# Branch A's queries and keys transposed two tiles at a time, and a later due time for the T5 set-up, in a hybrid encoder layer

## The chip, the cores and the metric

The kernel runs on one core of a Trainium2 chip. The metric is the device time of one execution in microseconds, as the median of several runs. A profiled execution gives the trace; its span goes from the first to the last instruction.

## The reference

One encoder layer is applied with the same weights to two inputs, a prompt of 512 tokens and a sample of 1024 tokens, 1024 wide, in f32. Cut to what matters here:

```python
h = rmsnorm(x, norm_g)
qa, ka, va, za, qb, kb, vb, zb, ga, gb = split(h @ w_in)
qa, ka = rmsnorm(qa per head, qn_a), rmsnorm(ka per head, kn_a)      # branch A: 8 heads of 64
oa = neighbourhood_attention(qa, ka, va, rpb_a) * silu(za)           # 8 x 16 window on a grid 64 wide
qb, kb = rmsnorm(qb per head, qn_b), rmsnorm(kb per head, kn_b)      # branch B: 8 heads, 2 key heads
ob = window_gqa_attention(qb, kb, vb, t5_table, sink_b) * silu(zb)   # |i-j| <= 128, T5 bias, sink logit
y = x + (sigmoid(ga) * (oa @ w_o_a) + sigmoid(gb) * (ob @ w_o_b)) @ w_out
```

## The kernel before

Every f32 product is made of three fp32r matmuls: an operand is split into a high part (an ACT copy to fp32r) and a low part (DVE or POOL subtract it), and hi x hi, hi x lo and lo x hi are added up in PSUM. The work goes in this order: norm of the prompt, attention of the prompt, its dense phase (gates, output projections, w_out), then attention and dense phase of the sample.

Tokens lie in tiles of 128: 4 for the prompt, 8 for the sample. An attention phase (`attention_phase`, line 648) goes through six groups: four of branch A with two heads each, two of branch B with four heads and one key head each. In a group, for each tile:

- `project` (line 728) makes queries, keys and values of the tile with 24 matmuls of 384 columns into one of two "p" banks (line 761). ACT squares (L780), DVE reduces (L785), POOL makes the reciprocal roots (L792, L799), ACT and DVE write the values in two parts into a tile `v` (L806, L809; 7 buffers for the sample, 6 for the prompt), and DVE scales queries and keys into `qk` (L816; 2 buffers).
- `make_qk` (line 847) transposes `qk` on PE into one "x" bank (line 861): two transposes of 128 columns for branch A (two heads' queries side by side, then their keys), three for branch B. Then ACT copies the keys with their gain (L882), DVE makes the low part (L887), ACT copies the queries (L896) and DVE makes their low part (L901). The prompt's branch A stores queries shifted by 64 tokens (`whole`), so that its first tile is written in two halves that lie apart.
- When the last tile that a block of 128 queries needs is there, the block waits in a list (line 1127); two blocks of branch A, or one of branch B, make a batch for `attend` (line 908): scores (L934), bias and running minimum on DVE (L969), exponentials on ACT (L978), scaling (L1008, L1010), transposes of the weights (L1026) and products with the values (L1063). A block of the sample reads the values of its own tile and both neighbours; one of the prompt, of two tiles.

`setup` (line 620), called on line 1644 with due time -0.7, loads the sink and makes its negative (L629), loads the T5 table and two constants (L634 to L636), makes the line of T5 biases by a matmul (L639) and a subtraction (L643), and stores it to DRAM (L646), from where branch B's groups load it (L708). The sink is named as an input of every score operation.

The order is written by a planner (`Flow.run`, line 207). Every operation has a list of engines with a fixed cost, a due time (`prio`) and what it depends on. The planner steps through time by these costs; an engine that is free takes, of the operations that are ready and whose buffers have room, the one with the lowest due time. What it finds is the order of each engine's queue. Loads and stores all go through SP's queue in that order, and a store waits there for its source. Branch A's due time is the running number of the tile in the phase; a group's weights are due 3 tiles before it.

Of the kernel before, what the change touches and what calls it, by code (L numbers as in the profile page):

```python
# [10 lines left out]
F32 = mybir.dt.float32  # L11
F32R = mybir.dt.float32r
AF = mybir.ActivationFunctionType
ALU = mybir.AluOpType
# [6 lines left out]
OADD = (("pool", 612), ("dve", 335))  # L21
DEBUG = 0
HB = 4
BANKS = {"p": 2, "x": 5, "d": 1}
ROTA = "ppxxxxxd"
FILL_P, FILL_S = 3, 2
# [14 lines left out]
P = 128  # L41
D = 1024
# [8 lines left out]
GW = 384  # L51
# [303 lines left out]
def encoder_kernel(  # L355
# [23 lines left out]
    nc = tc.nc  # L379
    act = nc.scalar  # L380
    dve = nc.vector
    pe = nc.tensor
# [7 lines left out]
    ident = cpool.tile([P, P], F32, tag="ident", name="ident")  # L390
# [25 lines left out]
    one = cpool.tile([1, P], F32, tag="one", name="one")  # L416
# [7 lines left out]
    ACT_ = lambda n, sbuf=True: (110 if sbuf else 68) + 0.832 * n  # L424
# [195 lines left out]
    def setup(pool, prio, after):  # L620
        raw = f.value(pool, [P, 8], F32, "sink_raw", 1)
        f.dma(lambda: nc.sync.dma_start(gcol, gains), 2048, -1, into=[gains_v])
        f.op(
            (("dve", 80),), lambda e: dve.tensor_scalar(gq, gcol[:, 0:2], -0.125, None, op0=ALU.mult),
            -1, use=[gains_v], into=[gains_v],
        )
        f.dma(lambda: nc.sync.dma_start(raw.t, sink.partition_broadcast(P)), 4096, prio, new=[raw], after=after)
        sink_v.writers.append(f.op(
            (("dve", 80),), lambda e: dve.tensor_scalar(nsink, raw.t, -1.0, None, op0=ALU.mult), prio, use=[raw]  # L629
        ))  # L630
        t5_sb = f.value(pool, [32, 8], F32, "t5_sb", 1)
        hot = f.value(pool, [32, 512], F32, "hot_sb", 1)
        far = f.value(pool, [8, 512], F32, "far_sb", 1)
        f.dma(lambda: nc.sync.dma_start(t5_sb.t, t5), 1024, prio, new=[t5_sb], after=after)  # L634
        f.dma(lambda: nc.sync.dma_start(hot.t, t5_hot), 65536, prio, new=[hot], after=after)
        f.dma(lambda: nc.sync.dma_start(far.t, t5_far), 16384, prio, new=[far], after=after)  # L636
        ps = bank("x")
        f.op(
            (("pe", 900),), lambda e: pe.matmul(ps.t[:8, :], t5_sb.t, hot.t, start=True, stop=True),  # L639
            prio, new=[ps], use=[t5_sb, hot],  # L640
        )
        f.op(
            (("dve", 602),), lambda e: dve.tensor_tensor(far.t, far.t, ps.t[:8, :], op=ALU.subtract),  # L643
            prio, use=[ps, far], into=[far],
        )
        line_op.append(f.dma(lambda: nc.sync.dma_start(line_d, far.t), 16384, prio, use=[far]))  # L646

    def attention_phase(geo, hh, hl, h_ops, mask_d, early, late):

        nb, nt = geo.nb, geo.nt  # L650
        kt = f.value(early, [P, 4, nt], F32R, "kt", 1)
        stores = {(c, n): [] for c in range(8) for n in range(nt // 512)}
        exps = []

        def tile_(shape, dt, tag, bufs):
            return f.value(early if tag in ("sq", "ss", "rs_v", "rs_r", "v", "q", "qt", "qk") else late, shape, dt, tag, bufs)
# [68 lines left out]
            o += i * GW if br == "B" else 0  # L725
            return nb_t.t[:, o : o + n]

        def project(br, w, t, prio):

            nq, nk = (2, 2) if br == "A" else (4, 1)  # L730
            nn = nq + nk
# [23 lines left out]
            for k in range(KC):  # L755
                hi, lo = w[k // 2]
                c = slice((k % 2) * GW, (k % 2) * GW + GW)
                for m, (u, mv) in enumerate(((0, hi), (0, lo), (1, hi))):
# [50 lines left out]
                lambda e: dve.tensor_tensor(vv(1), pv(), vv(0).bitcast(F32), op=ALU.subtract),  # L809
                prio, use=[ps, v], into=[v],  # L810
            )
            qk = tile_([P, GW], F32, "qk", 2)
            one = nn if br == "A" else nq
            f.op(
                (("dve", DVE_(one * 64)),),
                lambda e: dve.tensor_tensor(  # L816
                    qk.t[:, : one * 64].rearrange("p (h d) -> p h d", d=64),
                    ps.t[:, : one * 64].rearrange("p (h d) -> p h d", d=64),
                    r.t[:, :one].unsqueeze(2).to_broadcast([P, one, 64]),
                    op=ALU.mult,  # L820
                ),
                prio, new=[qk], use=[ps, r],
            )
            if br == "B":

# [18 lines left out]
            for j in range(nb)  # L844
        ]

        def make_qk(br, gi, t, qk, prio):

            npair = 1 if br == "A" else 2
            k0 = 2 * (gi % 2)  # L850
            pt = bank("x")
            whole = br == "A" and shifted
            if whole:
                q = q_whole.setdefault(gi, tile_([P, 2, nt + 64], F32R, "qt", 2))
            else:
                q = tile_([P, 2, 2 * P], F32R, "q", 4)
            fresh = not q.writers

            def emit(e):
                for i in range(npair + 1):  # L860
                    pe.transpose(pt.t[:, i * P : (i + 1) * P], qk.t[:, i * P : (i + 1) * P], ident)  # L861

            f.op((("pe", 110 * (npair + 1)),), emit, prio, new=[pt, q] if fresh else [pt], use=[qk])
            if fresh and not whole:
                q.writers.clear()
            n = npair * P
            pts = lambda: pt.t[:, :n]
            qv = lambda u: q.t[:, u, :n]
            if whole and t:
                qv = lambda u: q.t[:, u, t * P : (t + 1) * P]  # L870
# [4 lines left out]
            tok = slice(t * P, (t + 1) * P)  # L875
# [4 lines left out]
            a = f.op(  # L880
                (("act", ACT_(P) + 45),),
                lambda _: act.activation(kt.t[:, k0, tok], pk(), AF.Copy, scale=gain_k[br]),  # L882
                prio, use=[pt, gains_v], after=old, **kw,
            )
            b = f.op(
                (("dve", DVE_(P) + 165),),
                lambda _: dve.scalar_tensor_tensor(  # L887
                    kt.t[:, k0 + 1, tok], pk(), gain_k[br], kt.t[:, k0, tok].bitcast(F32), op0=ALU.mult, op1=ALU.subtract
                ),
                prio, use=[pt, gains_v], after=[a] + old, hold=[kt],  # L890
            )
            for s in slots:
                reads[s] = []
            c = f.op(
                (("act", ACT_(n) + 40),),
                lambda _: act.activation(qv(0), pts(), AF.Copy, scale=gain_q[br]),  # L896
                prio, use=[pt, gains_v], into=[q],
            )
            f.op(
                (("dve", DVE_(n) + 165),),  # L900
                lambda _: dve.scalar_tensor_tensor(  # L901
                    qv(1), pts(), gain_q[br], qv(0).bitcast(F32), op0=ALU.mult, op1=ALU.subtract
                ),
                prio, use=[pt], into=[q], after=[c],
            )
            return q, [a, b]

        def attend(br, gi, g, batch, nb_t, info, prio):
# [199 lines left out]
        for gi, (br, g) in enumerate(groups):  # L1108
# [524 lines left out]
    for t in range(gp.nb):  # L1633
# [4 lines left out]
        for i, (ps, users) in enumerate(gains_row if t == 0 else ()):  # L1638
# [133 lines left out]
```

## Time and profile before

| | us |
|---|---|
| median of 3 runs | 1148.09 (1146.76 to 1149.12) |
| profiled execution | 1146.52 |
| its span | 1144.7 |
| PE busy | 1133.8 |
| DVE busy | 854.4 |
| ACT busy | 644.9 |
| POOL busy | 308.3 |

A time beside an instruction counts from the start of the span. A matmul's row gives its start and its own duration, which overlaps with the next one's; the pace is read from start to start.

### The profile page before, as it was taken

The numbers are of one execution on the slowest core, as the hardware profiler recorded it, in microseconds if no ns is written. First come the engines' busy times: TensorE is split into PE (matmuls) and PEld (weight loads), VectorE is DVE, ScalarE is ACT, GpSimd is POOL, SyncE is SP. The second block draws the span as 40 slices with busy tenths as digits, with TensorE's granted clock in tenths as the row PEclk, the third lists the DMA queues.
The fourth block names the chain that finished last, engine by engine and source line by source line (L and its number), as shares of the span: only waits on it lengthen the run. The fifth ranks groups of instructions, "written<-read, shape, count | busy, mean of one in ns | idle before, by whom it ended". The sixth has DMA issues, their size and how long they took to land.

```text
span 1144.7 us, 18482 instructions
## 1 busy us (share of the span) xinstructions
PE 1133.8 (99%) x6139; PEld 985.8 (86%) x6139; DVE 854.4 (75%) x1975; ACT 644.9 (56%) x1467; POOL 308.3 (27%) x413
## 2 busy tenths in 40 slices
PE   8999999999999999999999999999999999999998
PEld 6999988888888899999999888888888888788887
DVE  5888798497765468887778888865878755497984
ACT  5777987544433346665678988865534434343320
POOL 3653433000010054343333445330222210132110
PEclk9999999999999999999999999999999999999999
DMA  7854543488786422121221213226657335573072
GB/s 253 273 158 141 181 113 102 115 264 266 232 277 199 165 72 67 25 70 32 71 61 50 56 37 93 56 66 214 218 148 211 129 111 159 200 238 121 29 223 90
DMA packets 124705, 159.86 MB, mean 140 GB/s; under 512 B 28297, under 2 KB 66961, under 8 KB 124610
## 3 DMA queue, kind: packets, MB, share of 16 engines
q1 hardware_dynamic: 124610, 158.69, 45.4%
q8 instruction: 48, 0.79, 0.3%
q14 instruction: 47, 0.39, 0.1%
HBM read 121.93 MB, written 41.44 MB: 143 GB/s over the span
## 4 chain that ended last, share of the span: by engine, by line
PE 94%; DVE 2%; DMA 2%; ACT 1%; POOL 1%; issue 0%; SPq 0%; ACTq 0%; POOLq 0%
PE p L761 25%; PE x L1285 9%; PE x L1286 9%; PE x L1284 9%; PE x L1063 5%; PE x L1026 5%; PE x L934 4%; PE p L1284 4%; PE p L1285 4%; PE d L1284 4%; PE p L1286 4%; PE d L1286 4%; PE d L1285 4%; PE x L861 2%; DMA ot<-u_d 1%; DMA w<-in_w_att_dram 1%
## 5 line engine op out<-in xcount | busy, mean ns | idle before, releaser
L761 PE MATMUL p<-whi,hh 128*128 128x384 f32 x384 | 133.4, 348 | 0.0
L761 PE MATMUL p<-wlo,hh 128*128 128x384 f32 x384 | 133.1, 347 | 0.0
L761 PE MATMUL p<-whi,hl 128*128 128x384 f32 x384 | 132.4, 345 | 0.0
L978 ACT ACTIVATE sb<-sb,mx 128x384 f32<-128x384 f32 (+1 forms) x192 | 107.5, 563 | 22.4 <-DVE mx L969 22.2
L1167 ACT ACTIVATE whi<-raw 128x512 fp32r<-128x512 f32 (+1 forms) x140 | 81.1, 590 | 52.6 <-PE x L1285 26.2
L761 PE MATMUL p<-whi,hb 128*128 128x384 f32 x384 | 107.5, 347 | 0.0
L1172 POOL TENSOR_TENSOR wlo<-raw,whi 128x512 fp32r<-128x512 f32 (+1 forms) x29 | 40.9, 1413 | 242.4 <-ACT whi L1167 130.4
L1284 PE MATMUL x<-hh,whi 128*128 128x512 f32 x264 | 102.7, 389 | 0.0
L1285 PE MATMUL x<-hl,whi 128*128 128x512 f32 x264 | 102.7, 389 | 0.0
L1286 PE MATMUL x<-hh,wlo 128*128 128x512 f32 x264 | 102.7, 389 | 0.0
L1037 DVE TENSOR_TENSOR pp<-x,pp 128x512 fp32r<-128x512 f32 (+1 forms) x136 | 82.6, 638 | 18.9 <-ACT pp L1032 17.8
L1172 DVE TENSOR_TENSOR wlo<-raw,whi 128x512 fp32r<-128x512 f32 (+1 forms) x111 | 70.1, 645 | 30.5 <-ACT whi L1167 30.2
L1285 PE MATMUL x<-T,whi 128*128 128x512 f32 x224 | 87.5, 390 | 0.3 <-DVE T L1172 0.2
L1286 PE MATMUL x<-T,wlo 128*128 128x512 f32 x224 | 87.2, 389 | 0.0
L1284 PE MATMUL x<-T,whi 128*128 128x512 f32 x224 | 87.1, 389 | 0.0
L1032 ACT ACTIVATE pp<-x 128x512 fp32r<-128x512 f32 (+1 forms) x136 | 70.9, 560 | 22.8 <-PE x L1026 21.8
L799 POOL TENSOR_TENSOR rs_r<-rs_v,mhalf 128x4 f32<-128x4 f32 (+1 forms) x72 | 81.7, 1134 | 5.7
L1063 PE MATMUL x<-pp,v 128*128 128x256 f32 (+1 forms) x368 | 77.8, 324 | 0.8 <-DVE pp L1037 0.8
L792 POOL TENSOR_SCALAR rs_v<-ss 128x4 f32<-128x4 f32 (+1 forms) x72 | 26.2, 364 | 187.3 <-DVE ss L785 184.6
L761 PEld LDWEIGHTS p<-whi,hl 128*128 128x128 f32 x384 | 73.0, 190 | 1.3 <-issue 1.0
L761 PEld LDWEIGHTS p<-wlo,hh 128*128 128x128 f32 x384 | 73.0, 190 | 1.0 <-issue 0.5
L761 PEld LDWEIGHTS p<-whi,hh 128*128 128x128 f32 x384 | 73.0, 190 | 0.9 <-issue 0.5
(351 smaller groups left out, 2985.5 us busy)
## 6 DMA issues: line engine op xcount, KB each, us to landing
raw<-in_w_g_dram SPq DMA_DIRECT2D x76, 256.0 KB
w<-in_w_att_dram SPq DMA_DIRECT2D x46, 384.0 KB
ot<-o_d SPq DMA_DIRECT2D x36, 256.0 KB
g_d<-C SPq DMA_DIRECT2D x34, 256.0 KB
raw<-in_w_z_dram SPq DMA_DIRECT2D x32, 256.0 KB
raw<-in_w_out_dram SPq DMA_DIRECT2D x32, 256.0 KB
C<-g_d SPq DMA_DIRECT2D x24, 256.0 KB
out_dram<-C SPq DMA_DIRECT2D x23, 256.0 KB
```

The costliest lines, as they stand in the source:

```text
L761: pe.matmul(ps.t[:, :GW], part[u](k), mv.t[:, c], start=k == 0 and m == 0, stop=k == KC - 1 and m == 2,)
L799: lambda e: nc.gpsimd.tensor_tensor(r.t[:, :nn], rv.t[:, :nn], mhalf[:, :nn], op=ALU.pow),
L978: act.activation(sb.t[:, :width], sb.t[:, :width], AF.Exp, bias=mx.t[:, i : i + 1], scale=-1.0, accum_out=sm.t[:, i : i + 1],)
L1026: pe.transpose(pt.t[:, u * P : (u + 1) * P], sbs[i].t[:, c * P : (c + 1) * P], ident)
L1032: lambda e, pt=pt, pp=pp, nn=nn: act.activation(pp.t[:, 0, :nn], pt.t[:, :nn], AF.Copy),
L1037: lambda e, pt=pt, pp=pp, nn=nn: dve.tensor_tensor(pp.t[:, 1, :nn], pt.t[:, :nn], pp.t[:, 0, :nn].bitcast(F32), op=ALU.subtract),
L1063: pe.matmul(out(), v.t[:, vs], mv(), start=first, stop=last)
L1167: (("act", ACT_(n)),), lambda e: act.activation(hi(), src(), AF.Copy), prio,
L1172: lambda e: engines[e].tensor_tensor(lo(), src(), hi().bitcast(F32), op=ALU.subtract), prio,
L1284: pe.matmul(out, hi.t[:, cs], mh(), start=first and k == 0, stop=False)
L1285: pe.matmul(out, hi.t[:, cs], ml(), start=False, stop=False)
L1286: pe.matmul(out, lo.t[:, cs], mh(), start=False, stop=last and k == len(ws) - 1)
```

## The change

Two neighbouring tiles of branch A share one `qk` tile of 512 columns, the second tile's queries and keys from column 256. The first tile of a pair is projected and no more; with the second, one run of four transposes follows (queries of both tiles, then keys of both), and one copy of 256 columns each for keys and queries in place of two of 128. For the prompt's first pair the query copy is in two parts, of 192 and 64 columns. Blocks that need either tile of the pair become ready with the second. The set-up is called with due time 9, and its two constants lie in one of the four `xt` buffers, which the norm uses, in place of two tiles of their own.

```diff
@@ setup
-        hot = f.value(pool, [32, 512], F32, "hot_sb", 1)
-        far = f.value(pool, [8, 512], F32, "far_sb", 1)
+        both = f.value(pool, [P, D], F32, "xt", 4)
+        hot, far = (lambda: both.t[:32, :512]), (lambda: both.t[:8, 512:1024])
...
-        line_op.append(f.dma(lambda: nc.sync.dma_start(line_d, far.t), 16384, prio, use=[far]))
+        line_op.append(f.dma(lambda: nc.sync.dma_start(line_d, far()), 16384, prio, use=[both]))
@@ project
-            qk = tile_([P, GW], F32, "qk", 2)
+            qk = beside or tile_([P, 512 if two else GW], F32, "qk", 2)
             one = nn if br == "A" else nq
+            c0 = 256 if beside else 0
...
-                    qk.t[:, : one * 64].rearrange("p (h d) -> p h d", d=64),
+                    qk.t[:, c0 : c0 + one * 64].rearrange("p (h d) -> p h d", d=64),
@@ make_qk
             def emit(e):
-                for i in range(npair + 1):
-                    pe.transpose(pt.t[:, i * P : (i + 1) * P], qk.t[:, i * P : (i + 1) * P], ident)
+                for i in range((npair + 1) * nt_):
+                    j = i // 2 + i % 2 * 2 if nt_ == 2 else i
+                    pe.transpose(pt.t[:, i * P : (i + 1) * P], qk.t[:, j * P : (j + 1) * P], ident)
...
-            n = npair * P
+            n, nk = npair * nt_ * P, nt_ * P
...
+            elif whole and nt_ == 2:
+
+                parts = [
+                    (lambda u: q.t[:, u, 64:n], lambda: pt.t[:, 64:n], n - 64),
+                    (lambda u: q.t[:, u, nt : nt + 64], lambda: pt.t[:, :64], 64),
+                ]
...
-            slots = [(s, t) for s in (k0, k0 + 1)]
+            tok = slice(t * P, t * P + nk)
+            slots = [(s, t + i) for i in range(nt_) for s in (k0, k0 + 1)]
...
-            pk = lambda: pt.t[:, n : n + P]
+            pk = lambda: pt.t[:, n : n + nk]
@@ attend
-                        at = runs[0][0] if whole else pair * P
+                        at = runs[0][0] if whole else runs[0][0] % (2 * P) if br == "A" and two else pair * P
@@ the loop over a group's tiles
-                v, qk = project(br, w, t, prio)
-                info[t] = (v, *make_qk(br, gi, t, qk, prio))
-                waiting += [b for b in (a_blocks if br == "A" else b_blocks) if max(b[1]) == t]
+                if br == "A" and two:
+                    if t % 2 == 0:
+                        v0, qk = project(br, w, t, prio)
+                        continue
+                    v, _ = project(br, w, t, prio, qk)
+                    made = make_qk(br, gi, t - 1, qk, prio, 2)
+                    info[t - 1], info[t], last = (v0, *made), (v, *made), (t - 1, t)
+                else:
+                    v, qk = project(br, w, t, prio)
+                    info[t], last = (v, *make_qk(br, gi, t, qk, prio)), (t,)
+                waiting += [b for b in (a_blocks if br == "A" else b_blocks) if max(b[1]) in last]
@@ the call
-    setup(norm_p, -0.7, h_ops["p"][1][:1])
+    setup(norm_p, 9, h_ops["p"][1][:1])
```

## Rows read from the trace of the kernel before

**Rows 1.** The page's part 1: busy us (share of the span) and instructions.

```profile
PE 1133.8 (99%) x6139; PEld 985.8 (86%) x6139; DVE 854.4 (75%) x1975; ACT 644.9 (56%) x1467; POOL 308.3 (27%) x413
```

**Rows 2.** The page's part 4: the chain that ended last, by engine.

```profile
PE 94%; DVE 2%; DMA 2%; ACT 1%; POOL 1%; issue 0%; SPq 0%; ACTq 0%; POOLq 0%
```

**Rows 3.** Stretches: length, busy time and instructions of each engine, granted clock, DMA.

```profile
core 0: us, PE busy (x) PEld busy (x) DVE busy (x) ACT busy (x) POOL busy (x), PEclk, DMA share, GB/s
0.00:31.00 31.00, 25.11 (x117) 21.51 (x118) 18.31 (x46) 18.76 (x37) 13.47 (x23) 1.00 0.74 251
...
403.00:617.00 214.00, 213.19 (x1417) 201.57 (x1416) 170.88 (x514) 135.53 (x368) 84.98 (x120) 1.00 0.20 55
```

**Rows 4.** The chain in order of time: start us, us, what.

```profile
50.59 4.18 PE p L761 x24
```

**Rows 5.** PE's waits: line, releaser, us in total, times, longest.

```profile
PE x L861 <- DVE qk L816: 1.0, 2, 0.5
```

**Rows 6.** PE's timeline at the two waits: start, us, what [idle before].

```profile
30.87 0.41 PE L861 MATMUL x<-ident,qk 128*128 128x128 f32 x2 [0.50 <-DVE qk L816]
...
404.16 0.44 PE L861 MATMUL x<-ident,qk 128*128 128x128 f32 x2 [0.52 <-DVE qk L816]
```

**Rows 7.** PE's timeline around a run of four transposes and one of two.

```profile
27.74 0.60 PE L532 MATMUL x<-ident,xt 128*128 128x128 f32 x4
...
28.35 0.34 PE L761 MATMUL p<-wlo,hh 128*128 128x384 f32 x1
...
36.00 0.38 PE L861 MATMUL x<-ident,qk 128*128 128x128 f32 x2
36.14 0.42 PE L761 MATMUL p<-whi,hh 128*128 128x384 f32 x1
36.40 0.33 PE L761 MATMUL p<-wlo,hh 128*128 128x384 f32 x1
```

**Rows 8.** Groups by line and shape, ACT and DVE: busy us, mean ns | idle before.

```profile
L882 ACT ACTIVATE kt<-x,gcol 128x128 fp32r<-128x128 f32 x72 | 26.3, 366 | 35.1 <-PE x L861 34.6
L896 ACT ACTIVATE q<-x,gq 128x256 fp32r<-128x256 f32 x24 | 11.3, 471 | 0.0
...
L887 DVE SCALAR_TENSOR_TENSOR kt<-x,gcol,kt 128x128 fp32r<-128x128 f32 x72 | 24.9, 345 | 14.4 <-ACT q L896 12.9 <-ACT qt L896 1.2
L901 DVE SCALAR_TENSOR_TENSOR q<-x,gq,q 128x256 fp32r<-128x256 f32 x24 | 11.3, 472 | 0.0
```

**Rows 9.** The timeline at the set-up of sink and T5 line, all engines.

```profile
12.41 0.58 SPq L627 DMA_DIRECT2D sink_raw<-in_sink_dram  x1
...
14.49 0.28 SPq L636 DMA_DIRECT2D far_sb<-in_t_far_dram  x1
...
23.61 0.17 DVE L629 TENSOR_SCALAR nsink<-sink_raw 128x8 f32<-128x8 f32 x1
...
23.67 1.02 PE L639 MATMUL x<-hot_sb,t_sb 32*8 32x512 f32 x2
...
25.02 0.67 DVE L643 TENSOR_TENSOR far_sb<-far_sb,x 8x512 f32<-8x512 f32 x1
...
25.71 0.30 SPq L646 DMA_DIRECT2D line_d<-far_sb  x1
```

**Rows 10.** SP's waits up to 60 us: releaser, us in total, times, longest.

```profile
SPq L646 <- DVE ss L785: 8.3, 1, 8.3
```

**Rows 11.** PE's timeline at the end of a sample group of branch A.

```profile
441.15 1.31 PE L934 MATMUL x<-kt,q 64*128 64x384 f32 x12
...
447.02 0.38 PE L861 MATMUL x<-ident,qk 128*128 128x128 f32 x2
...
453.43 0.63 PE L1063 MATMUL x<-pp,v 128*128 128x256 f32 x4
...
464.83 0.38 PE L861 MATMUL x<-ident,qk 128*128 128x128 f32 x2
```

More of the change, by code (lines that the diff above doesn't have):

```diff
@@ L23 @@
 HB = 4
+TWO = {512: True, 1024: True}
 BANKS = {"p": 2, "x": 5, "d": 1}
@@ L631, in setup @@
         t5_sb = f.value(pool, [32, 8], F32, "t5_sb", 1)
-        hot = f.value(pool, [32, 512], F32, "hot_sb", 1)
-        far = f.value(pool, [8, 512], F32, "far_sb", 1)
+        both = f.value(pool, [P, D], F32, "xt", 4)
+        hot, far = (lambda: both.t[:32, :512]), (lambda: both.t[:8, 512:1024])
         f.dma(lambda: nc.sync.dma_start(t5_sb.t, t5), 1024, prio, new=[t5_sb], after=after)
-        f.dma(lambda: nc.sync.dma_start(hot.t, t5_hot), 65536, prio, new=[hot], after=after)
-        f.dma(lambda: nc.sync.dma_start(far.t, t5_far), 16384, prio, new=[far], after=after)
+        f.dma(lambda: nc.sync.dma_start(hot(), t5_hot), 65536, prio, new=[both], after=after)
+        f.dma(lambda: nc.sync.dma_start(far(), t5_far), 16384, prio, into=[both], after=after)
         ps = bank("x")
         f.op(
-            (("pe", 900),), lambda e: pe.matmul(ps.t[:8, :], t5_sb.t, hot.t, start=True, stop=True),
-            prio, new=[ps], use=[t5_sb, hot],
+            (("pe", 900),), lambda e: pe.matmul(ps.t[:8, :], t5_sb.t, hot(), start=True, stop=True),
+            prio, new=[ps], use=[t5_sb, both],
         )
         f.op(
-            (("dve", 602),), lambda e: dve.tensor_tensor(far.t, far.t, ps.t[:8, :], op=ALU.subtract),
-            prio, use=[ps, far], into=[far],
+            (("dve", 602),), lambda e: dve.tensor_tensor(far(), far(), ps.t[:8, :], op=ALU.subtract),
+            prio, use=[ps, both], into=[both],
         )
-        line_op.append(f.dma(lambda: nc.sync.dma_start(line_d, far.t), 16384, prio, use=[far]))
+        line_op.append(f.dma(lambda: nc.sync.dma_start(line_d, far()), 16384, prio, use=[both]))
     def attention_phase(geo, hh, hl, h_ops, mask_d, early, late):
         nb, nt = geo.nb, geo.nt
+        two = TWO[nt]
         kt = f.value(early, [P, 4, nt], F32R, "kt", 1)
@@ L726, in bias_of, with project @@
             return nb_t.t[:, o : o + n]
-        def project(br, w, t, prio):
+        def project(br, w, t, prio, beside=None):
             nq, nk = (2, 2) if br == "A" else (4, 1)
@@ L821, in project @@
                 ),
-                prio, new=[qk], use=[ps, r],
+                prio, use=[ps, r], **({"into": [qk]} if beside else {"new": [qk]}),
             )
@@ L845, in attention_phase, with make_qk @@
         ]
-        def make_qk(br, gi, t, qk, prio):
+        def make_qk(br, gi, t, qk, prio, nt_=1):
             npair = 1 if br == "A" else 2
@@ L859, in emit @@
             def emit(e):
-                for i in range(npair + 1):
-                    pe.transpose(pt.t[:, i * P : (i + 1) * P], qk.t[:, i * P : (i + 1) * P], ident)
-            f.op((("pe", 110 * (npair + 1)),), emit, prio, new=[pt, q] if fresh else [pt], use=[qk])
+                for i in range((npair + 1) * nt_):
+                    j = i // 2 + i % 2 * 2 if nt_ == 2 else i
+                    pe.transpose(pt.t[:, i * P : (i + 1) * P], qk.t[:, j * P : (j + 1) * P], ident)
+            f.op((("pe", 110 * (npair + 1) * nt_),), emit, prio, new=[pt, q] if fresh else [pt], use=[qk])
             if fresh and not whole:
                 q.writers.clear()
-            n = npair * P
+            n, nk = npair * nt_ * P, nt_ * P
             pts = lambda: pt.t[:, :n]
             qv = lambda u: q.t[:, u, :n]
+            parts = [(qv, pts, n)]
             if whole and t:
-                qv = lambda u: q.t[:, u, t * P : (t + 1) * P]
+                parts = [(lambda u: q.t[:, u, t * P : t * P + n], pts, n)]
+            elif whole and nt_ == 2:
[3 more added lines that the diff above has]
+                ]
             elif whole:
@@ L874, in make_qk @@
                 qv = lambda u: q.t[:, u, 64:].rearrange("p (a n) -> p a n", n=64)[:, :: nt // 64 - 1]
-            tok = slice(t * P, (t + 1) * P)
-            slots = [(s, t) for s in (k0, k0 + 1)]
+                parts = [(qv, pts, n)]
+            tok = slice(t * P, t * P + nk)
+            slots = [(s, t + i) for i in range(nt_) for s in (k0, k0 + 1)]
             old = [o for s in slots for o in reads.get(s, ())]
             kw = {"hold": [kt]} if reads else {"new": [kt]}
-            pk = lambda: pt.t[:, n : n + P]
+            pk = lambda: pt.t[:, n : n + nk]
             a = f.op(
-                (("act", ACT_(P) + 45),),
+                (("act", ACT_(nk) + 45),),
                 lambda _: act.activation(kt.t[:, k0, tok], pk(), AF.Copy, scale=gain_k[br]),
@@ L885, in make_qk @@
             b = f.op(
-                (("dve", DVE_(P) + 165),),
+                (("dve", DVE_(nk) + 165),),
                 lambda _: dve.scalar_tensor_tensor(
@@ L893, in make_qk @@
                 reads[s] = []
[L894 to L905, printed above, removed]
+            for qv, pts, m in parts:
+                c = f.op(
+                    (("act", ACT_(m) + 40),),
+                    lambda _, qv=qv, pts=pts: act.activation(qv(0), pts(), AF.Copy, scale=gain_q[br]),
+                    prio, use=[pt, gains_v], into=[q],
+                )
+                f.op(
+                    (("dve", DVE_(m) + 165),),
+                    lambda _, qv=qv, pts=pts: dve.scalar_tensor_tensor(
+                        qv(1), pts(), gain_q[br], qv(0).bitcast(F32), op0=ALU.mult, op1=ALU.subtract
+                    ),
+                    prio, use=[pt], into=[q], after=[c],
+                )
             return q, [a, b]
```

## Prediction

> **What bounds the kernel now.** I read the busy table first: TensorE's matmuls cover 99% of the span, its weight loads 86% [rows 1]. A busy share alone is not a bound, so the chain that ended last comes next: 94% of it is PE, 2% DVE, 1% ACT [rows 2]. Then the stages: from 403 to 617 us, where the sample's four branch A groups run, PE idles 214.00 - 213.19 = 0.81 us, while DVE is busy 170.88 us (80%) and ACT 135.53 (63%); in the first 31 us PE idles 5.9 us [rows 3]. Last, whether a busy PE is also a fast one: 24 projection matmuls of 384 columns follow each other in 4.18 us, 174 ns each [rows 4], and the granted clock is 1.00 in the stages listed [rows 3]. That is 384 columns at 2.4 GHz (160 ns) and 14 ns more. So PE is full nearly everywhere; time is won only where PE waits, or by instructions that PE need not run. The waits that name the transposes of the change are two, 1.0 us together, both for the DVE's scaling into qk [rows 5].
>
> By the Trainium skill (Perfetto Trace Analysis, Identifying the Most-Contended Engine) matmul busy time says little of how near TensorE is to its limit, and the share of weight loads says more; by it the 86% would leave 14% open. The 174 ns here speak against room of that size.
>
> **The change, part by part.**
>
> *Transposes.* Branch A has 16 + 32 = 48 tiles, so 48 runs of two 128-column transposes become 24 runs of four. The number of transposes stays 96. What a run costs is read from start to start, up to the second matmul behind it (the first is stretched), less one matmul of 0.174. A run of two: 36.40 - 36.00 - 0.174 = 0.226 us. A run of four at another line: 28.35 - 27.74 - 0.174 = 0.436 [rows 7]. Two runs of two less one of four: 0.016 us; times 24 pairs -0.4 us. The rows round to 10 ns, so this lies between 0 and -0.8; I take -0.3.
>
> *The two waits.* At 30.87 the transposes of the prompt's second tile waited 0.50 us, at 404.16 those of the sample's first tile 0.52 [rows 6]. In the second case PE stood in front of a ready projection, because the run of the first tile was issued before it. After the change the first tile of a pair issues no transposes, so the next projection follows at once, and the run comes when its first half is long done. Late next is the second half, scaled by DVE at the end of the same chain; the hand-made planner then lets a projection go first if it thinks the run not ready. Bounds: -1.0 (both go) to +1.0 (as much waits elsewhere, since a planned order that is off by half a microsecond is what made these two). I take -1.0, since 22 of the 24 pairs sit in stretches where none of these runs waits now.
>
> *Copies.* Per pair ACT loses two operations and DVE two. A key copy of 128 columns takes 366 ns on ACT and 345 on DVE; a query copy of 256, which branch B has, 471 and 472 [rows 8]. Taking the query copies of 128 as equal to the key copies, and key copies of 256 as equal to branch B's query copies, a pair saves 2 x (2 x 366 - 471) = 522 ns on ACT and 2 x (2 x 345 - 472) = 436 on DVE: 24 times that is 12.5 and 10.5 us. The prompt's first pair of each of the four groups keeps its query copy in two parts (192 and 64 columns), which gives back about 0.31 us (64 columns, by the slope between these rows) on each engine four times. None of it is on PE's path. What hides it is the projection matmuls, 4.2 us per tile; without that cover the stage would follow DVE (a rival below).
>
> *Later attention.* Scores of a batch now wait for the odd tile. Sample batches ready behind tiles 2, 4, 6, 7 become ready behind 3, 5, 7, 7; the prompt's behind 2, 3 become 3, 3. PE has projections of the next tiles and groups in hand meanwhile, so I cost this at nothing. If the cover goes, it is because tiles run out, the third rival.
>
> *Set-up of the T5 line and the sink.* Four loads on SP's queue (from 12.41 to 14.49), a DVE operation of 0.17 us on the sink, a matmul in two passes (1.02 us) on PE at 23.67, a DVE subtraction of 0.67 us, and the store of the line at 25.71 get due time 9 instead of -0.7 [rows 9]. Everything is still done: PE's 1.02 us moves from a place where the next norm transposes queue behind it to one where PE is full. Price 0; bounds -1.0 (it falls into a hole) and +0.1 (what the matmul behind such a switch is stretched by, 36.40 - 36.14 - 0.174 [rows 7]). On SP the store waited 8.3 us for DVE, with weight and bias loads queued behind it [rows 10]; that wait moves too. From 31 us on PE idles for no load, so I cost both ends at nothing. The sink operation is also an input of every score, branch A's too, by the planner's books; at due time 9 the first scores could be held until DVE has a free slot. The loads of tables and weights with earlier due times go ahead on SP, some six at 0.3 to 0.6 us, 2 to 4 us against first scores that come after 40 us: nothing, or up to +1 if DVE finds no slot. The loads also pass the fill weights in SP's queue, and the T5 constants take one of four x buffers, that the sample's norm statistics load into; those are due much later.
>
> **Sum.** -0.3 (runs) - 1.0 (waits) + 0 (copies, order, T5) = -1.3 us. The profiled execution took 1146.52 us (span 1144.7 and 1.8 around it), so it would be 1145.2. The median of the three runs shown, 1148.09, is 1.6 above it; for the median I forecast 1146.8. About 0.2% (2.3 us) is what a measurement of this kernel can tell from no change.
>
> **Rivals.**
>
> *A: the waits come back.* The order is planned from fixed costs, so another tile may wait. For: both waits are errors of that plan by half a microsecond. Against: half as many runs. Then -0.3 remains: 1147.8. That would also be the time if the "later" set-up is not later: the planner takes a due time only as an order among ready operations.
>
> *B: DVE's relief comes through.* If PE's full rows hide slack, stages follow DVE. In 403 to 617 us DVE is 80% busy [rows 3], and the sample saves 16 x 0.436 = 7.0 us there; 80% of it is 5.6 us: 1148.1 - 5.6 = 1142.5. Against: 174 ns per matmul and 0.81 us of idle time in 214. The page named above would support this case, by its 14%.
>
> *C: slower, by the value tiles.* The sample has 7 buffers for v (line 777), freed when the last block that reads them is through. Now a batch scored at 441.15 ends its product at 453.43 + 0.63, 12.9 us later; the last tile of the group is transposed at 447.02 and the third of the next group at 464.83 [rows 11]. The batch of blocks 4 and 5 then starts after 447.02, say at 448.5, and ends at 461.4. At that time five v tiles of the old group and two of the next are held, and the third of the next, written some 3 us before its transposes (461.8, an estimate), needs one of them. So the margin is about 0.4 us, and behind it stands the second projection bank, worth one more projection of 4.2 us. From a slip of 4.6 us PE stops. If two batches ready at once slip by half a batch, 6.4 us, it stops 1.8 us at each of the sample's four group ends: +7.2 - 1.3 = +5.9, so 1154.0; at a slip of 5.5 us it is +2.3. Against: the planner knows the buffers and would score earlier where it can.
>
> The Trainium skill (Perfetto Trace Analysis, Optimization Strategy) says that a gap that repeats on the engine that should be full can mean too few buffers; it is how C would look. No such gap is in the rows of before.
>
> **How the numbers follow.** Forecast 0.50, A 0.17, B 0.18, C 0.15. Faster by more than 0.2% (below 1145.8): B, and 0.10 of the forecast, where T5 falls into a hole (-1.0 more): 0.28. Slower: C, 0.15. Within: 0.57. Forecast and A alone span 1145.4 to 1149.0 (bounds of waits, T5 and sink). To leave out no more than 2 in 10, the range takes in most of B (down to 1142.6) and C up to a slip of about 5.5 us: 1142.6 to 1150.4.
>
> **What would show it.** Right: 24 runs of four and 24 of the old three-transpose runs at the transposes' line; no idle PE in front of those of 31 and 404 us; ACT 12 and DVE 10 us less busy; matmul share still 99%; the T5 matmul after 25 us. Wrong: a stage from 403 to 617 that shrinks by several microseconds with PE's matmuls no closer (B), or PE idle time repeating at group ends, released by the value copy or the projection's bank (C). If PE's total idle time falls by more than 3 us, my reading of where PE can still win is wrong.

## The result and the profile after

The changed kernel took 1149.39 us (median of 20 runs, 1147.41 to 1154.93). The kernel before, run beside it, took 1146.9 (median of 20). The ratio is 1.0022, with a 95% interval of 1.0013 to 1.0032: slower by about 2.5 us, where 1.3 us less was forecast. The profiled execution took 1149.98 us (span 1148.2), 3.5 us more than that of before. Of the kernels below, one execution (2900.93 us, the delay in both stages) counts as slow and is left out of its ratio.

Part 1 of the page and the first line of part 4, kernel after, as [rows 1, 2]:

```profile
PE 1134.7 (99%) x6139; PEld 986.6 (86%) x6139; DVE 849.5 (74%) x1933; ACT 642.9 (56%) x1432; POOL 294.1 (26%) x402
...
PE 95%; DMA 2%; DVE 1%; ACT 1%; issue 1%; POOL 0%; SPq 0%; ACTq 0%; DVEq 0%; POOLq 0%
```

Nothing in these two lines tells of the loss. PE is busy 99% in both kernels. The stages tell more. First the kernel before, the prompt's attention (a stretch that [rows 3] leave out):

```profile
31.00:217.00 186.00, 186.00 (x1174) 167.57 (x1174) 151.80 (x446) 145.83 (x368) 78.91 (x126) 1.00 0.50 152
```

Then the kernel after, with the two stages of [rows 3] around the same stretch (columns as there):

```profile
0.00:31.00 31.00, 24.58 (x119) 20.85 (x119) 18.52 (x44) 20.15 (x37) 13.00 (x24) 1.00 0.89 296
...
31.00:217.00 186.00, 183.76 (x1154) 164.92 (x1153) 147.65 (x424) 140.92 (x353) 81.83 (x132) 1.00 0.47 141
...
403.00:617.00 214.00, 213.64 (x1400) 202.14 (x1399) 160.18 (x465) 128.48 (x322) 76.77 (x114) 1.00 0.21 61
```

Before, PE has no idle time at all in the 186 us of the prompt's attention. After, it lacks 2.24 us there. It lacks 0.53 us more than before in the first 31 us, and gains 0.45 in the sample's branch A. ACT and DVE are less busy in the stretch that lost, so neither became the bound.

PE's waits, kernel after (line, releaser, us in total, times, longest), as [rows 5]:

```profile
PE p L763 <- DVE qk L819: 1.6, 2, 1.3
PE d L1306 <- DVE fc L1515: 1.1, 2, 0.8
...
PE p L763 <- DVE v L811: 0.7, 1, 0.7
...
PE x L948 <- DVE kt L900: 0.3, 1, 0.3
```

The transposes (now line 866) are in the list no more. In their place projections (763) wait for a bank that DVE has yet to read, and scores (948) wait for the second half of a key copy. Three of these waits (1.3, 0.7 and 0.3 us) lie in the prompt's attention and make up the 2.24 us. The fills' 1.1 us (1306) and the remaining 0.3 of the projections lie in the sample, where PE waited 1.6 us before.

**Where the prompt's time went.** The chain of waits, followed back from the end, by line in the stretch from 58 to 96 us. First the kernel before, whose chain there is PE alone:

```profile
by line: PE p L761 68.1%; PE x L1063 8.0%; PE x L934 7.1%; PE x L1026 5.9%; PE x L861 3.8%; PE d L1285 2.5%; PE d L1286 2.4%; PE d L1284 2.4%
```

The kernel after, the same stretch: pieces of the chain in order of time (start us, us, what):

```profile
65.05 5.29 DMA w<-in_w_att_dram
70.36 0.85 ACT whi L603
71.28 0.84 issue
72.12 0.49 DVE kt L900
72.65 0.38 PE x L948 x2
73.04 0.38 PE x L948 x2
...
75.54 0.91 PE x L948 x12
...
84.37 4.13 DMA o_d<-ot__1222
88.60 0.61 ACT ot__1298 L1084
89.28 0.73 POOL ot__1298 L1090
...
90.10 0.44 POOL rs_v L794
...
90.61 1.79 POOL rs_r L801
92.42 0.43 DVE qk L819
...
92.99 2.53 PE p L763 x13
```

Read it downwards. A weight load is issued at 65.05 and lands at 70.34. ACT's split of those weights (603) stands in its queue ahead of the key copy of a pair, whose transposes began at 67.58, and ACT idles 3.66 us in front of it (timeline, [idle before]):

```profile
70.36 0.84 ACT L603 ACTIVATE whi<-w 128x768 fp32r<-128x768 f32 x1 [3.66 <-DMA w<-in_w_att_dram]
```

So DVE's key copy ends only at 72.6, and the scores behind it start late. Four of them take 0.76 us, where twelve at 75.54 take 0.91. The second piece has the same form with another cause. ACT's copy of an attention output (1084) waits for its buffer until an earlier output's store, issued at 84.37, is done. Behind it POOL, also in order, is late with the output's sum (1090), then with the projection's scale (794, 801); DVE scales the bank late; PE's next projection starts at 92.99 after 1.26 us of waiting. Most of these instructions are late because of what stands ahead of them in their engine's queue, not because they are long. POOL's two scale operations are long as well: 1.79 us, where the median of the 72 of line 801 is 1.02, and 0.44 us, where that of line 794 is 0.20. With the medians the wait of 1.26 us would be about 0.25, by an estimate from these figures (spans on POOL are rough). What made them long wasn't taken apart.

**The steps that could be seen.** Timeline of PE, kernel after, at the places of [rows 6]:

```profile
30.54 0.66 PE L866 MATMUL x<-ident,qk 128*128 128x128 f32 x4
...
407.86 0.41 PE L763 MATMUL p<-whi,hh 128*128 128x384 f32 x1 [0.35 <-DVE qk L819]
...
411.44 0.60 PE L866 MATMUL x<-ident,qk 128*128 128x128 f32 x4
```

Both waits are gone, as forecast; a projection at 407.86 now waits 0.35 us. ACT's copies, groups by line and shape, as [rows 8]:

```profile
L910 ACT ACTIVATE q<-x,gq 128x256 fp32r<-128x256 f32 x40 | 18.9, 472 | 0.0
L895 ACT ACTIVATE kt<-x,gcol 128x256 fp32r<-128x256 f32 x24 | 11.4, 473 | 17.5 <-PE x L866 17.5
L895 ACT ACTIVATE kt<-x,gcol 128x128 fp32r<-128x128 f32 x24 | 8.8, 367 | 5.8 <-PE x L866 5.6
L910 ACT ACTIVATE qt<-x,gq 128x256 fp32r<-128x256 f32 x4 | 1.9, 466 | 0.0
L910 ACT ACTIVATE qt<-x,gq 128x192 fp32r<-128x192 f32 x4 | 1.7, 429 | 0.0
L910 ACT ACTIVATE qt<-x,gq 128x64 fp32r<-128x64 f32 x4 | 1.3, 314 | 0.0
```

They add up to 44.0 us. The set-up, timeline of the kernel after, as [rows 9]:

```profile
27.75 0.45 DVE L630 TENSOR_SCALAR nsink<-sink_raw 128x8 f32<-128x8 f32 x1
...
29.59 1.02 PE L640 MATMUL x<-xt,t_sb 32*8 32x512 f32 x2
...
32.26 0.66 DVE L644 TENSOR_TENSOR xt<-xt,x 8x512 f32<-8x512 f32 x1
...
34.31 0.44 SPq L647 DMA_DIRECT2D line_d<-xt  x1
```

The matmul comes 5.9 us later than before, the store 8.6 us.

### The profile page after: what moved, and what is told of

It is laid out like the page before. It is cut to its first block, busy times and chain, and to the rows that moved or that the text cites. A ratio compares the mean times of both kernels' runs of the same rounds, so it can differ in the third digit from the quotient of the medians.

```text
span 1148.2 us, 18400 instructions
## 1 busy us (share of the span) xinstructions
PE 1134.7 (99%) x6139; PEld 986.6 (86%) x6139; DVE 849.5 (74%) x1933; ACT 642.9 (56%) x1432; POOL 294.1 (26%) x402
## 4 chain that ended last, share of the span: by engine, by line
PE 95%; DMA 2%; DVE 1%; ACT 1%; issue 1%; POOL 0%; SPq 0%; ACTq 0%; DVEq 0%; POOLq 0%
PE p L763 25%; PE x L1307 9%; PE x L1308 9%; PE x L1306 9%; PE x L1077 5%; PE x L948 5%; PE x L1040 5%; PE d L1306 4%; PE p L1307 4%; PE p L1306 4%; PE p L1308 4%; PE d L1308 4%; PE d L1307 4%; PE x L866 2%; DMA w<-in_w_att_dram 1%
## 5 line engine op out<-in xcount | busy, mean ns | idle before, releaser
L763 PEld LDWEIGHTS p<-whi,hb 128*128 128x128 f32 x384 | 68.9, 188 | 4.1 <-issue 1.5
```

The lines of the kernel that those rows point to most:

```text
L763: pe.matmul(ps.t[:, :GW], part[u](k), mv.t[:, c], start=k == 0 and m == 0, stop=k == KC - 1 and m == 2,)
```

## The experiments

Three theories. **Delay**: the prompt's scores, held until the fourth tile, bring their work on ACT, DVE and POOL together and late. **Set-up**: the later sink and T5 line cost what was costed at nothing. **Order**: any edit that changes the planned order of the queues in the prompt costs, whichever it is.

**The set-up alone, both ways of holding its constants.** The first kernel is the changed one without pairs (constants in an x buffer); the second is the kernel before with one number changed.

```
-TWO = {512: True, 1024: True}
+TWO = {512: False, 1024: False}
```

> Pairs off in both phases; only the set-up at due time 9 with its constants in an x buffer. Theory 1 (the prompt's pairs: scores of both batches ready at once, DVE, POOL and SP's queue fall behind, PE waits for a projection bank): ratio 0.999 to 1.001, no PE wait over 0.5 us between 60 and 100 us. Theory 2 (the set-up: it takes an x buffer and reorders SP's queue, weights come late): 1.002 to 1.003, with the waits at 64, 72 and 91 us still there. Theory 3 (the planned order is as good as chance, any edit moves the time by a few us): anything from 0.998 to 1.003, with waits at other places.

```
-    setup(norm_p, -0.7, h_ops["p"][1][:1])
+    setup(norm_p, 9, h_ops["p"][1][:1])
```

> The kernel before with the set-up at due time 9, constants in their own tiles. If a taken x buffer is what costs in the run of the set-up alone (1.0053): 0.999 to 1.001 here. If the planned order scatters with any edit: between 0.998 and 1.006, and where it is slow, a wait in the dense phase of the prompt, which the set-up has nothing to do with.

Measured: 1.0053 (1.0036 to 1.0070) and 1.0057 (1.0037 to 1.0077), about 6 us slower each. The first is slower than any theory had it. So the x buffer is not the cause; the due time is. In the first, PE's busy time falls by 1.11 us in the prompt's attention and by 3.17 in the dense phase behind it (217 to 403 us); in the second by 5.18 and 2.55. Timeline of PE and of ACT in the second kernel:

```profile
363.07 0.63 ACT L1167 ACTIVATE hh<-C 128x512 fp32r<-128x512 f32 x1 [2.12 <-DVE C L1161]
...
363.76 0.50 PE L1284 MATMUL x<-hh,whi 128*128 128x512 f32 x1 [2.33 <-ACT hh L1167]
```

and one stretch of the first kernel (columns as [rows 3]):

```profile
360.00:370.00 10.00, 8.50 (x29) 6.62 (x30) 3.99 (x7) 2.74 (x5) 0.00 (x0) 0.83 0.67 206
```

A later due time for a few small instructions near 20 us thus brings a stall of 2.3 us near 360 us; the plan of everything behind them is another one. In the first kernel the granted clock is 0.83 in the ten microseconds with its stall of 2.32 us, so some of them ran at 1.2 GHz; in the second it is 1.00 in the same stretch. The changed kernel has no such stall: the cost of the set-up alone isn't a term that can be added.

**The set-up's due time, and its halves.** The same line of the kernel before with 3; the sink alone at 9; the T5 line alone at 9.

> The kernel before with the set-up of the T5 line and the sink at due time 3 in place of -0.7, own tiles, nothing else: a measure of how far the planned order moves the time. If only the late place of the set-up costs (by 9 it is +6 us), this lies between, +1 to +3 us. If every new order does, it can be anywhere from -2 to +6, and not on a line between the two.

> The kernel before with only the sink's load and its DVE operation at due time 9; the T5 line stays at -0.7. The prediction's theory: nothing, at most +1 us (first scores wait for DVE to find a slot). If the sink is the half that costs, 1150 or more (ratio 1.004 to 1.006). If neither half alone matters but any new order does, this and the run with the line alone both come out slower, by unlike amounts and at unlike places.

> The kernel before with only the T5 line (three loads, the matmul, the subtraction, the store) at due time 9; the sink stays at -0.7. The prediction's theory: -1.0 to +0.1 us. If this half costs, 1150 or more. If any new order costs, slower too, but not the sum with the other half (4.5 to 6.5 us).

Measured: 1.0039 (1.0027 to 1.0051), 1.0031 (1.0017 to 1.0045) and 1.0039 (1.0026 to 1.0052). Each half costs, and due time 3 costs about as much as either. The halves' sum, 1.0070, can't be told from the whole's 1.0057 (1.0037 to 1.0077), so these runs don't show whether they add up. The sink's half is one load and a DVE operation of 0.17 us [rows 9], and costs 3.6 us: that speaks for order and against the set-up's instructions being dear. In the changed kernel, due time 5 in place of 9 made no difference:

> The whole change with the set-up at due time 5 in place of 9. Prompt's pairs as the cause: 1.0015 to 1.003, with PE idle or late between 50 and 130 us as in the changed kernel. Scatter of the plan: from 0.998 to 1.005, the loss elsewhere or gone.

Measured: 1.0023 (1.0013 to 1.0034).

**The pairs, by stage.** The first has pairs in the prompt only, set-up at 9; the second in the sample only, set-up as before.

```
+TWO = {512: True, 1024: False}
```

> Pairs in the prompt only, set-up at 9. Theory 1: 1.002 to 1.003, as the whole change, and the loss before 130 us. Theory 2: 1.002 to 1.003 as well. Theory 3: anywhere.

```
+TWO = {512: False, 1024: True}
```

> Pairs in the sample only, set-up as before. Theories 1 and 2: 0.999 to 1.000, PE's progress over the sample's attention (403 to 770 us) at most 0.5 us from that of before. Theory 3: up to 0.3% either way.

Measured: 1.0018 (1.0009 to 1.0027), nearly all of the change's loss, and 1.0000 (0.9991 to 1.0009). Two thirds of the pairs bring nothing net. The prompt's pairs ran only with the late set-up; no run has them with the set-up as before, so their own share of the 1.0018 is not known.

**The delay without pairs or set-up.** In the kernel before, the batches of branch A behind an even tile wait for the odd one; first in both stages, then in one (`or nt != NT_P`, then `or nt != NT_S`, added behind `br == "B"`). The held batch's due time moves by one tile with it, as it does with pairs.

```
-waiting += [b for b in (...) if max(b[1]) == t]
+last = (t,) if br == "B" else (t - 1, t) if t % 2 else ()
+waiting += [b for b in (...) if max(b[1]) in last]
```

> The kernel before, transposes and copies per tile as they were, but branch A's blocks become ready only behind odd tiles, as with pairs. Theory 1 in its form that the later, clumped batches do it: 1.002 to 1.003, with waits for a projection bank in the prompt's branch A groups. If instead the wide copies or the four-transpose runs do it: 0.999 to 1.001. Theory 3: anywhere.

> The kernel before with the prompt's batches behind tile 2 held until tile 3, nothing else (runs of two, narrow copies, set-up as before). Theory 1 (delay): the whole loss of the kernel with the delay in both stages, 3 to 4 us slower than before, 1149 to 1150. Theory 2 (set-up): within 1 us of before.

> The kernel before with the sample's branch A batches behind tiles 2, 4, 6 held until tiles 3, 5, 7, nothing else. Theory 1 (holding a batch costs in the sample too): 1.0008 to 1.002, which is what the sample's pairs lack against the same pairs with no batch held (1.0000 against 0.9984). Theory 2 (the sample's eight tiles give cover, the prompt's four do not): within 0.5 us of before, and the difference of those two kernels is one of order.

Measured: 1.0034 (1.0021 to 1.0047) in both stages, 1.0043 (1.0031 to 1.0056) in the prompt, 1.0002 (0.9990 to 1.0014) in the sample. Holding a batch costs in the prompt and nothing in the sample. The prompt's attention, first with the delay in the prompt:

```profile
31.00:217.00 186.00, 183.41 (x1151) 164.17 (x1150) 144.20 (x405) 143.96 (x359) 93.76 (x147) 1.00 0.47 149
```

then with the delay in the sample:

```profile
31.00:217.00 186.00, 185.96 (x1169) 166.93 (x1168) 149.99 (x441) 144.83 (x365) 77.28 (x124) 1.00 0.50 151
```

The kernel with the delay in the prompt loses its time elsewhere than the changed kernel, from about 140 us on (2.28 of its 2.59 us), but in a like way. Its timeline:

```profile
143.57 0.62 ACT L662 ACTIVATE bias<-raw 128x384 f32<-128x384 f32 x1 [1.12 <-DMA raw<-line_d]
...
148.01 0.58 ACT L1494 ACTIVATE fc<-d 128x512 f32<-128x512 f32 x1
...
148.65 0.50 PE L1285 MATMUL d<-hh,fh 128*128 128x512 f32 x1 [1.59 <-ACT fc L1494]
```

ACT stands 1.12 us at a bias table that hasn't landed, then works off casts and exponentials, and comes to the eviction that PE's fill matmuls need 1.59 us too late.

**The suspected queues one by one.** In the changed kernel, a third buffer for the attention's outputs in the prompt (ACT's wait at 88.60); then the prompt's weights due one step sooner (the load at 65.05).

```
-            ot = tile_([P, 4, P], F32, "ot_", 2)
+            ot = tile_([P, 4, P], F32, "ot_", 3 if nt == NT_P else 2)
```

> The whole change with three output buffers in the prompt in place of two. If the two batches that become ready together wait for an output buffer whose store has not landed (ACT 1.3 us at 88.6, POOL behind it, and so qk and the projection bank at 91): the wait of 1.26 us at 92.99 goes, ratio 1.0005 to 1.0015. If late weights are the cause: as the changed kernel, 1.0015 to 1.003.

```
-                    w_att[gi, i], 768, lead - 3 if gi else -8 + i,
+                    w_att[gi, i], 768, lead - (4 if nt == NT_P else 3) if gi else -8 + i,
```

> The whole change with the prompt's attention weights due four tiles ahead in place of three. Late weights as the cause (ACT waits 9.9 us for them between 31 and 130 us, 5.6 before): ACT's wait for weights back to about 5 us and 1.0000 to 1.0012. Output buffers as the cause: 1.0015 to 1.003.

Measured: 1.0016 (1.0005 to 1.0027), within the uncertainty of the change's own 1.0022, and 1.0040 (1.0026 to 1.0055). With the third buffer the wait of 1.26 us is gone, and PE's busy time in the prompt's attention rises from 183.76 to 184.96 us; in the dense phase behind it, it falls from 186.00 to 185.17. The time lies between what the two causes were expected to give and decides for neither. In the change with the set-up at 5 this wait is absent too, and its time is the change's (1.0023). ACT's wait for weights from 31 to 130 us, kernel after:

```profile
ACT whi L603 <- DMA w<-in_w_att_dram: 9.9, 6, 3.8
```

and with the weights due sooner:

```profile
ACT whi L603 <- DMA w<-in_w_att_dram: 3.4, 3, 1.3
...
ACT junk L461 <- DMA xt<-in_x_s_dram: 1.8, 1, 1.8
```

The edit did what it was made for: 6.5 us of waiting for weights went away, and the time didn't fall (1.0040 against 1.0022; the two intervals overlap). The Trainium skill (Perfetto Trace Analysis, Optimization Strategy) says to look for the gaps of the engine that one optimizes and to make what it waits for start sooner, or complete faster. PE's wait of 0.27 us at the scores hung on those weights and is gone too; the measurement decides, and the time didn't follow. ACT now waits 1.8 us for an input tile of the sample, which it didn't in the change: it seems that one load went sooner and others later.

**Pairs that hold no batch.** Two tiles are still run together, but the pairs are chosen so that each batch is ready behind the same tile as before: the prompt as (0,1), 2, 3, the sample as (0,1), 2, (3,4), (5,6), 7.

```
+FIRST = {512: (0,), 1024: (0, 3, 5)}
...
-                if br == "A" and two:
-                    if t % 2 == 0:
-                        v0, qk = project(br, w, t, prio)
-                        continue
+                if br == "A" and two and t in FIRST[nt]:
+                    v0, qk = project(br, w, t, prio)
+                    continue
+                if br == "A" and two and t - 1 in FIRST[nt]:
                     v, _ = project(br, w, t, prio, qk)
...
```

First in both stages with the set-up at 9, then in the sample alone with the set-up as before, then as the first with the sink back at -0.7.

> The changed kernel, set-up at 9 too, but with the pairs laid so that no batch of scores waits longer than in the kernel before: the prompt's tiles run as (0,1), 2, 3 and the sample's as (0,1), 2, (3,4), (5,6), 7 (28 runs in place of 48). Theory 1 (the delay of the prompt's batches behind tile 2 costs the 3 us between 60 and 130 us): that loss is gone, 31 to 124 us holds about as much matmul time of PE as the kernel before (92.5 or more of 93), time 1146 to 1147. Theory 2 (the later set-up of the T5 line and the sink, or any new order, costs it, whatever the pairs): the loss stays or comes elsewhere, 1148.5 or more, perhaps with a stall of 2.3 us near 360 us as in the two kernels with the late set-up and no pairs.

> The kernel before, set-up as before, with pairs only in the sample, and there as (0,1), 2, (3,4), (5,6), 7: no batch waits longer. If the delay gave back what the sample's pairs won (they came to 1.0000), this is 1.0 us faster than the kernel before, 1145.0. If what was won is lost to the planned order anyway, it is within 0.5 us of it.

> The changed kernel with pairs that hold no batch (prompt (0,1), 2, 3; sample (0,1), 2, (3,4), (5,6), 7), the T5 line at due time 9 and the sink back at -0.7. If the sink's late place costs, 2 us or more faster than the same kernel with the sink at 9 (1.0009), 1143 to 1145. If any new order counts, anywhere from 1143 to 1149.

Measured: 1.0009 (0.9995 to 1.0023); 0.9984 (0.9976 to 0.9993); 1.0061 (1.0048 to 1.0073). The first seems to get back more than half of the change's loss, but this doesn't confirm the theory of delay. Its expectation had PE busy for 92.5 us or more of the 93 from 31 us on (before 93.00, the change 90.79), and the trace has 91.71:

```profile
31.00:124.00 93.00, 91.71 (x594) 85.84 (x594) 73.95 (x227) 68.84 (x176) 46.92 (x79) 1.00 0.56 180
```

Its pairs in the sample are other ones too, and the second kernel shows what those bring alone: 0.0016, more than the 0.0013 between the first and the change. The second is faster than both kernels: 1144.19 us, against 1145.7 beside it. The sample's stages in one stretch, with its pairs as in the change:

```profile
403.00:770.00 367.00, 365.64 (x2358) 335.87 (x2359) 289.91 (x820) 257.77 (x643) 133.52 (x198) 1.00 0.21 56
```

and with the pairs that hold no batch:

```profile
403.00:770.00 367.00, 367.00 (x2382) 337.41 (x2381) 296.10 (x844) 262.82 (x664) 130.37 (x196) 1.00 0.21 56
```

The first leaves PE 1.36 us idle in the sample's attention (1.1 of it where two fill matmuls wait for DVE's eviction), the second nothing. Before, PE idled 1.60 us there: 0.81 up to 617 us [rows 3], and 0.79 behind:

```profile
617.00:770.00 153.00, 152.21 (x950) 133.19 (x949) 127.20 (x337) 127.06 (x308) 63.98 (x98) 1.00 0.24 59
```

That is about the second kernel's gain. Holding the sample's batches alone cost nothing, though, so the difference is one of order, not of delay; what in the order makes it was not taken apart.

The third is the strongest test of order. It puts the sink back where it was, which the sink's own cost would have made a gain, and it is 6 us slower than its twin. Its timeline:

```profile
88.60 1.06 ACT L462 ACTIVATE junk<-xt 128x1024 bf16<-128x1024 f32 x1 [2.49 <-DMA xt<-in_x_s_dram]
89.65 0.37 ACT L783 ACTIVATE sq<-p 128x256 f32<-128x256 f32 x1
...
90.05 0.42 DVE L788 TENSOR_REDUCE ss<-sq 128x4 f32<-128x256 f32 x1 [2.91 <-ACT sq L783]
...
92.81 0.42 DVE L820 TENSOR_TENSOR qk<-p,rs_r 128x256 f32<-128x256 f32 x1 [0.90 <-POOL rs_r L802]
```

and PE's waits:

```profile
PE x L867 <- DVE qk L820: 4.2, 2, 2.5
```

ACT stood 2.49 us at a norm statistic of the sample, a stage that begins at 403 us, since its tile hadn't landed. The square of a prompt's projection stood behind it, and PE's transposes behind that.

All kernels together, by what they touch (PE's busy time from 31 to 217 us is of one profiled execution each; before 186.00):

| kernel | ratio | PE busy of 186 us |
|---|---|---|
| **nothing changed in the prompt** | | |
| pairs in the sample | 1.0000 | 185.94 |
| delay in the sample | 1.0002 | 185.96 |
| pairs in the sample, no batch held | 0.9984 | 186.00 |
| **prompt's order changed** | | |
| no batch held, set-up 9 | 1.0009 | 184.71 |
| changed kernel, third output buffer | 1.0016 | 184.96 |
| pairs in the prompt, set-up 9 | 1.0018 | 184.86 |
| the change | 1.0022 | 183.76 |
| the change, set-up 5 | 1.0023 | 184.93 |
| sink at 9 | 1.0031 | 182.59 |
| delay in both stages | 1.0034 | 182.82 |
| set-up at 3 | 1.0039 | 182.87 |
| T5 line at 9 | 1.0039 | 184.04 |
| the change, weights sooner | 1.0040 | 184.41 |
| delay in the prompt | 1.0043 | 183.41 |
| set-up at 9 in an x buffer | 1.0053 | 184.89 |
| set-up at 9 | 1.0057 | 180.82 |
| no batch held, sink back | 1.0061 | 180.75 |

In the first three kernels PE, ACT, DVE and POOL run the same instructions in the same order as before in the first 230 us, and PE stays full in the prompt's attention. In all fourteen kernels where it is another, PE loses 1.0 to 5.3 us, whatever the edit was. The column doesn't follow the ratio closely: some kernels lose time in the dense phase too, as the set-up at 9 in an x buffer does, and the profiled execution of "sink at 9" (1153.28 us) was the slowest of its seven, whose median is 1148.71. The time of "no batch held, set-up 9" can't be told from that of before.

## Why the prediction was wrong

- **What bounds the kernel** was read rightly: PE. The matmul's spacing held (24 in 4.19 us), and rival B didn't come: from 403 to 617 us DVE is 10.7 us less busy and PE 0.45 more. The rule under B (the Trainium skill, Perfetto Trace Analysis, Identifying the Most-Contended Engine) would have made the 14% beside the weight loads' 86% a reserve; no run here shows one.
- **Runs of four** cost 0.441 us in the median of 20 in the trace of the kernel after, read as in the prediction, and runs of two 0.221 in that of before: the term is about 0, at the edge of its bounds, not -0.3.
- **The two waits** went as forecast; that no others would come did not. "22 of the 24 pairs sit in stretches where none of these runs waits now" looked at waits of the transposes alone. In the prompt's attention PE waits 2.3 us at projections and scores, where it had waited 0.5 at the transposes, just ahead of 31 us. In the sample it waits 1.4 us at fills and a projection, where it had waited 1.6 in all. So rival A's mechanism came nearly in full in the sample, and in the prompt at more than four times the size of the wait that went.
- **Copies**: ACT's cost 55.1 us before (four groups of its two lines, of which [rows 8] show two) and 44.0 after, 11.1 less against 11.3 forecast (12.5 less four times 0.31). ACT as a whole is only 2.0 us less busy and DVE 4.9, where 12 and 10 were named as the sign, in part since the planner moved work: DVE took over 11 scalings of weights and three splits from POOL, whose busy time fell by 14.2, and ACT six scalings of `qk` and two evictions from DVE. The forecast also summed durations, and those of neighbours on ACT overlap: in the kernel after, a key copy from 71.11 lasts 0.46 us, and the query copy behind it starts at 71.47. How much each takes was not taken apart. That none of it would show on PE holds for the sample.
- **Later attention**, "I cost this at nothing", is the first step that failed. In the sample nothing is what it costs (1.0002). In the prompt, 4 tiles per group and both batches behind the last, it costs 1.0043 by itself, 5 us. The cover named, PE's projections in hand, did not suffice: it was operations on ACT, DVE and POOL, on which PE's banks depend, that came late (the eviction before 148.65, 1.59 us).
- **Set-up**, price 0 with bounds -1.0 and +0.1 (the sink up to +1), is the second: 6 us alone, 3.6 to 4.5 for either half. The step counted each instruction and each queue passed, and found nothing dear in it; no run shows one of them to be dear. It didn't count that the planner lays all that follows anew.
- **The sum** is the third. It adds terms, and they don't add: 5 us for the delay and 6 for the set-up make 2.5 together. The forecast's own price for the pairs' runs, 0.3, is far from the missing 8.5. Whether ACT's and DVE's relief gives some of it back in the prompt is not shown, since no run has the prompt's pairs with the set-up as before; that two of these edits together make a third order is a reading that fits the runs, not one that they prove.
- **The number** 1146.8 started from 1148.09, a median of three runs; over 20 the kernel before takes 1146.9, as if the change did nothing. 1149.39 lies inside the range given, 1142.6 to 1150.4, but by luck: the range reaches up so far for rival C, which didn't happen.
- **Rival C** had the sign, but not the place: no wait of PE for a value tile shows in the sample. Its price was 5.9 us; that its lesser case, 2.3, comes near the measured 2.5 is luck. The wait for a projection's bank that it named came in the prompt.

Shown: that the changed kernel's loss lies in the prompt's stages, mostly its attention, that either the delay or the set-up alone makes one there, and that the two don't add. Seen in the traces, but not shown to set the time: queues whose head waits for a transfer. The two edits that took such a wait away, the third output buffer and the sooner weights, didn't bring the time back. Not shown: why the order of the kernel before is the one that fits. Every other order of the prompt tried here costs PE time in it, and whether one exists that does not is open.

## What to carry to other kernels

Where the bound engine has no idle time in a stage and the other engines' queues are laid out ahead, price an edit there by what it does to the order, not by its instructions: here every new order of that stage cost PE 1.0 to 5.3 us in it, and the times rose by up to 7 us, while holding and pairing in the sample, with eight tiles to a group in place of four, cost nothing. Before grouping work, ask which consumer the group makes wait, and try groups that end where the consumers' batches end: in the sample such pairs came to 0.9984, the others to 1.0000. Test an edit's parts alone, but don't add up their prices.

## What was not expected

- A matmul of 1.02 us, two small DVE operations, four loads and a store, given a later due time near 20 us, brought a stall of 2.33 us at 363.76.
- Taking 6.5 us of ACT's waits for weights away didn't make the kernel faster (1.0040 against 1.0022), and putting one small operation and its load back to their old due time made it 6 us slower (1.0061 against 1.0009).
- A wait of scores shows up as idle time only in part (0.3 us in PE's waits); the rest looks like long matmuls, four in 0.76 us, where twelve take 0.91. Of the 3.5 us between the two profiled spans, PE's busy time up to 1140 us explains 2.53 (1132.17 against 1129.64).
